# SwiGLU feed-forward of an encoder layer: seven products of half-matrix sums in place of eight, and a down projection of its own

## The chip, the cores and the metric

One core of a Trainium2 chip. The metric is the device time of one execution in microseconds (us), median of several runs. The engines of the core are TensorE (PE; its weight loads are listed as PEld), VectorE (DVE), ScalarE (ACT), GpSimd (POOL) and SyncE (SP), which only issues DMAs here. POOL issues DMAs too, on a queue of its own.

## The reference

One layer of a bidirectional encoder, in fp32, on 1536 tokens of 1024 channels: a prompt of 1024 tokens and a sample of 512 with the same weights.

```python
h  = rms_norm(x)                       # then w_in, two kinds of attention with 8 heads each
x  = x + concat(oA, oB) @ w_out
h2 = rms_norm(x)
x  = x + (silu(h2 @ w_gate) * (h2 @ w_up)) @ w_down     # 1024 -> 2816 -> 1024
y  = rms_norm(x)
```

## The kernel before

Every fp32 product is made of three passes in a faster fp32 format of PE: an operand is split into a high part (ACT rounds it, L125) and a low part (the operand less the high part, on DVE or POOL, L126), and `mm3` (L151 to L159, the matmul itself is L156) adds high x high, high x low and low x high in one bank of PSUM. PSUM has eight banks; `bank(kind, ...)` takes one of those that a kind shares.

The program runs in stages: projections and attention, interleaved, until some 812 us; the out-projection, tile by tile of 128 tokens, which also puts the residual into DRAM (`x2_d`, L837) and the norm's scale into `rs2`; then the feed-forward and the final norm. The change touches the last stage, from L942 on.

The feed-forward has two chunks of 768 tokens. `h2_tile` (L956) loads a tile of the residual, scales it (L963), transposes it on PE and splits it into `hh` and `hl`, [128, 8, 768]: channels on partitions, eight blocks of them. The first chunk's six tiles are made during the out-projection, the second's inside the first chunk's down projection. Then `gate_up(ck, f)` (L997 on) runs over the 22 blocks f of 128 hidden channels: weight tiles of 128 x 8 x 128 for gate and up, and for each half of the chunk (384 tokens) 8 x 3 matmuls of 384 columns for gate and as many for up, so 96 per block. ACT makes the silu (L1019), DVE multiplies (L1020), and the result is split into `hidh` and `hidl` (L1021, L1022), which stay in SBUF. After each group of two or three blocks (`GROUPS`), `down` (L1035 on) multiplies them by their rows of w_down: per tile of 128 tokens and half of the output (512 columns) 9 or 6 matmuls, and DVE adds the bank into the residual tile `x` (L1042). The weights come on POOL's queue (L137: gate and up, two units ahead; L987: w_down), and are loaded for each chunk. `finish` (L1044 on) is the final norm of a tile and its store on SP's queue (L1058, L1060).

The order on each engine is set by the program order of these calls and a scheduler that follows the tiles' dependences: an instruction waits on semaphores for its operands and for the buffers that its pool rotates. An engine works off its own instructions strictly in order, and so does each DMA queue's issuer.

## Time and profile before

| | us |
|---|---|
| median of 3 runs | 2038.98 |
| lowest and highest | 2035.26, 2049.47 |
| profiled execution: span of the trace | 2041.9 |
| first to last matmul of the feed-forward | 925.92 to 2032.23 |

Only the span is known of the profiled execution; it is 2.9 us above the median. Instructions are placed in us from the span's start. A matmul's listed duration overlaps that of its neighbours, so the pace of a run of matmuls is read from the distance of their starts. "Idle before" is time in which the engine stood still ahead of an instruction, with what ended it.

### The profile page before, as it was taken

What the parts mean: (1) busy time and instruction counts of PE and PEld (TensorE: products, weight loads), DVE (VectorE), ACT (ScalarE), POOL (GpSimd) and SP (SyncE); (2) the same over time, 40 slices, a digit from 0 to 9 for tenths busy, and PEclk for the clock granted to TensorE, in tenths of its full rate; (3) what the DMA queues carried; (4) which work ended last, traced back from release to release, by engine and by line L of the source; (5) the groups of instructions that cost most, each with busy time, mean ns of one, the idle gap of its engine ahead of it and who ended that gap; (6) DMA issues with size and microseconds to landing.
All of it is one profiled execution on the core that took longest, in us unless ns stands there. A gap on an engine that the chain in (4) does not pass through costs nothing.

```text
span 2041.9 us, 27504 instructions
## 1 busy us (share of the span) xinstructions
PE 1965.3 (96%) x10408; PEld 1662.7 (81%) x10408; DVE 1013.4 (50%) x2217; ACT 772.9 (38%) x1414; POOL 413.9 (20%) x445
## 2 busy tenths in 40 slices
PE   6999989999999979999999999999999999999998
PEld 5666666666666657889999999999899999999997
DVE  6566756667756676654333333333553333333325
ACT  5565655655566575443121121122331221221122
POOL 3323333343455521001010010010010100110100
PEclk9989998999999879999999999999999999999999
DMA  7788897898898897527122121221252211221201
GB/s 253 160 178 152 165 183 132 177 148 154 156 192 172 172 211 190 186 101 249 43 82 62 57 78 52 63 73 62 81 188 62 73 62 63 63 64 61 62 21 62
DMA packets 314293, 243.09 MB, mean 119 GB/s; under 512 B 259872, under 2 KB 271280, under 8 KB 314160
## 3 DMA queue, kind: packets, MB, share of 16 engines
q1 hardware_dynamic: 281424, 122.04, 29.6%
q0 software_dynamic: 32736, 119.30, 20.2%
q8 instruction: 81, 1.33, 0.3%
q14 instruction: 52, 0.43, 0.1%
HBM read 159.85 MB, written 21.14 MB: 89 GB/s over the span
## 4 chain that ended last, share of the span: by engine, by line
PE 86%; DMA 8%; DVE 2%; ACT 2%; issue 1%; SPq 1%; POOL 0%; DVEq 0%; ACTq 0%; POOLq 0%
PE acc L156 76%; DMA pT<-p 5%; PE sc L692 4%; PE pv L760 3%; PE sc L691 2%; DMA vna<-va 1%; PE pt L214 1%; ACT ka L504 0%; DMA bias_e<-in_rpbf_dram 0%; DMA taba<-e_d 0%; DVE p L745 0%; DMA wo_raw<-in_w_out_dram 0%; DVE htl L293 0%; DVE kb L508 0%; DMA x_sq<-in_x_prompt_dram 0%
## 5 line engine op out<-in xcount | busy, mean ns | idle before, releaser
L156 PE MATMUL acc<-hh,whi 128*128 128x384 f32 x1408 | 478.4, 340 | 0.0
L156 PE MATMUL acc<-hh,wlo 128*128 128x384 f32 x1408 | 474.9, 337 | 0.0
L156 PE MATMUL acc<-hl,whi 128*128 128x384 f32 x1408 | 474.5, 337 | 0.0
L156 PEld LDWEIGHTS acc<-hh,whi 128*128 128x128 f32 x1408 | 264.3, 188 | 0.6
L156 PEld LDWEIGHTS acc<-hl,whi 128*128 128x128 f32 x1408 | 264.3, 188 | 0.5
L156 PEld LDWEIGHTS acc<-hh,wlo 128*128 128x128 f32 x1408 | 264.7, 188 | 0.1
L156 PE MATMUL acc<-hth,whi 128*128 128x512 f32 x576 | 243.9, 424 | 3.4 <-ACT hth L290 1.5
L156 PE MATMUL acc<-htl,whi 128*128 128x512 f32 x576 | 241.2, 419 | 0.5 <-DVE htl L293 0.2
L125 ACT ACTIVATE whi<-wraw 128x1024 fp32r<-128x1024 f32 x136 | 143.5, 1057 | 258.1 <-PE acc L156 249.3
L156 PE MATMUL acc<-hth,wlo 128*128 128x512 f32 x576 | 241.1, 419 | 0.2 <-POOL wlo L126 0.2
L156 PE MATMUL acc<-wdh,hidh 128*128 128x512 f32 x528 | 206.0, 390 | 0.0
L156 PE MATMUL acc<-wdl,hidh 128*128 128x512 f32 x528 | 205.5, 389 | 0.0
L156 PE MATMUL acc<-wdh,hidl 128*128 128x512 f32 x528 | 205.5, 389 | 0.0
L1042 DVE TENSOR_TENSOR x<-acc,x 128x512 f32<-128x512 f32 x168 | 115.8, 690 | 164.5 <-PE acc L156 164.3
L1020 DVE TENSOR_TENSOR sl<-acc,sl 128x384 f32<-128x384 f32 x88 | 49.1, 557 | 280.2 <-PE acc L156 280.2
L739 ACT ACTIVATE t<-t,mt 128x768 f32<-128x768 f32 (+3 forms) x192 | 137.5, 716 | 124.2 <-DVE mt L732 121.3
L126 DVE TENSOR_TENSOR wlo<-wraw,whi 128x1024 fp32r<-128x1024 f32 x88 | 107.8, 1225 | 151.4 <-ACT whi L125 151.1
L745 DVE SCALAR_TENSOR_TENSOR p<-t,p 128x768 f16<-128x768 f32 (+3 forms) x192 | 145.5, 764 | 72.2 <-ACT p L741 71.8
L126 POOL TENSOR_TENSOR wlo<-wraw,whi 128x1024 fp32r<-128x1024 f32 x48 | 118.6, 2474 | 176.1 <-ACT whi L125 151.8
L741 ACT ACTIVATE p<-t 128x768 f16<-128x768 f32 (+3 forms) x192 | 118.1, 624 | 84.0 <-DMA pT<-p 54.4
L125 ACT ACTIVATE wdh<-wdr 128x1024 fp32r<-128x1024 f32 x44 | 45.3, 1054 | 273.4 <-PE acc L156 265.4
L156 PEld LDWEIGHTS acc<-hth,whi 128*128 128x128 f32 x576 | 113.0, 196 | 36.9 <-issue 9.2
(139 smaller groups left out, 2794.1 us busy)
## 6 DMA issues: line engine op xcount, KB each, us to landing
wraw<-in_w_in_dram POOLq DMA_DIRECT2D x46, 512.0 KB, 5.9
wraw<-in_w_gate_dram POOLq DMA_DIRECT2D x44, 512.0 KB, 4.5
wraw<-in_w_up_dram POOLq DMA_DIRECT2D x44, 512.0 KB, 4.5
wdr<-in_w_down_dram POOLq DMA_DIRECT2D x44, 512.0 KB, 4.2
tabb<-in_tabb_dram POOLq DMA_DIRECT2D x8, 800.0 KB, 6.2
x_d<-x_res SPq DMA_DIRECT2D x12, 512.0 KB
xh<-x_d SPq DMA_DIRECT2D x12, 512.0 KB
x<-x_d SPq DMA_DIRECT2D x12, 512.0 KB
```

The costliest lines, as they stand in the source:

```text
L125: return (nc.scalar.activation(hi, src, AF.Copy), eng.tensor_tensor(out=lo, in0=src, in1=hi.bitcast(F32), op=ALU.subtract))
L126: eng.tensor_tensor(out=lo, in0=src, in1=hi.bitcast(F32), op=ALU.subtract))
L156: latest[0] = nc.tensor.matmul(out=out, lhsT=a, rhs=b, start=i == 0, stop=i == last)
L214: nc.tensor.transpose(out=pts[k // 4][:, k % 4 * P:(k % 4 + 1) * P], in_=src[:, k * P:(k + 1) * P], identity=ident)
L691: nc.tensor.matmul(out=out, lhsT=qh[:, qs], rhs=kx, start=True, stop=False)
L692: nc.tensor.matmul(out=out, lhsT=qh[hs, qs], rhs=lx, start=False, stop=True)
L739: nc.scalar.activation(t, t, AF.Exp, bias=mt, scale=-1.0, accum_out=k.den)
L741: nc.scalar.activation(k.p16[:, 0], t, AF.Copy, scale=16384.0)
L745: nc.vector.scalar_tensor_tensor(out=k.p16[:, 1], in0=k.t, scalar=16384.0, in1=k.p16[:, 0], op0=ALU.mult, op1=ALU.subtract)
L760: nc.tensor.matmul(start=j + i == 0, stop=j + i == m, **one)
L1020: nc.vector.tensor_tensor(out=sl, in0=accs[1], in1=sl, op=ALU.mult)
L1042: nc.vector.tensor_tensor(out=xs[b][:, z], in0=acc, in1=xs[b][:, z], op=ALU.add)
```

## The change

A product of two matrices, each cut into 2 x 2 blocks, takes eight products of blocks; Strassen's scheme (here in Winograd's form) takes seven, of sums and differences of the blocks, and adds their results. Both matrix products of the feed-forward are rewritten so.

- Gate and up: the rows are the two halves of the 1024 channels, the columns of the weight matrix gate and up, the columns of the activations two halves of 384 tokens of the chunk. A step `u` is one block f of one chunk. Its seven products of 4 x 3 matmuls are issued in the order 1, 6, 2, 7, 5, 4, 3 into banks `mm`, `y` and `z` (two of each). POOL forms four weight sums per step (`w_sum`, L1046 on; tile `fs`), and ACT and DVE split seven weight blocks (L1061 is the low part). `h_sum` makes the seven activation operands of a chunk once (`h1h`, `h1l` to `h7h`, `h7l`; 128 x 1536 each, the low part on DVE at L1006, the sums on POOL). DVE adds the banks to the gate and up results.
- The weights come on SP's queue (`fw_load`), in three buffers `fraw` that gate and up share.
- After every second step POOL forms the sums of the hidden activations that the down projection wants (tile `as`, L1144), and SP writes all seven of them to DRAM (`hid_d`, L1145): 128 x 21 x 128, 1.38 MB in pieces of 512 bytes.
- The down projection runs after all steps: seven products, in the order 1, 7, 6, 4, 5, 2, 3, each over six pairs of token tiles b and eleven pairs of hidden blocks j, 33 matmuls of 512 columns per (n, b). The hidden operand is read back (`hraw`, 0.72 MB) and split again; pieces of w_down (`wq`, 256 KB, four buffers) come on SP's queue, are summed on POOL where the product wants it (`diff`), and split. Results are added into the residual tiles, which are loaded at the start (`x2`, twelve of 512 KB). `finish` follows for one tile of a pair in product 5, for the other in product 3.
- The pool of the old weights is released before the feed-forward.

```diff
-GROUPS = (3, 3, 3, 3, 3, 3, 2, 2)
-    wp = ctx.enter_context(tc.tile_pool(name="wp", bufs=1))
+    wp = tc.alloc_tile_pool(name="wp", bufs=1)
-    def mm3(out, ops):
+    def mm3(out, ops, first=True):
...
-                latest[0] = nc.tensor.matmul(out=out, lhsT=a, rhs=b, start=i == 0, stop=i == last)
+                latest[0] = nc.tensor.matmul(out=out, lhsT=a, rhs=b, start=first and i == 0, stop=i == last,
+                                              skip_group_check=not first)
...
-    kinds.update(mm=("mm", 2), pv=("pv", 2), dn=("dn", 4))
+    kinds.update(mm=("mm", 2), y=("y", 2), z=("z", 2), dn=("dn", 2))
...
+    def h_sum(n):
+        hi = hpool[n].tile([P, 4, HC], F32R, tag=f"h{n}h", name=f"h{n}h")
+        lo = hpool[n].tile([P, 4, HC], F32R, tag=f"h{n}l", name=f"h{n}l")
+        b11, b12, b21, b22 = raw[0, 0], raw[0, 1], raw[1, 0], raw[1, 1]
...
+        elif n == 5:
+            src = mix(b12, b22, b11, ALU.subtract)
+        elif n == 4:
+            src = mix(b21, b21, b11, ALU.subtract)
...
+        nc.scalar.activation(hi, src, AF.Copy)
+        nc.vector.tensor_tensor(out=lo, in0=src, in1=hi.bitcast(F32), op=ALU.subtract)
...
+    def fw_load(u):
...
+                t = fw.tile([P, NK, P], F32, tag="fraw", name="fraw", bufs=3)
+                nc.sync.dma_start(out=t, in_=w[:, f * P:(f + 1) * P].rearrange("(k p) f -> p k f", p=P))
...
+    def w_sum(u):
...
+        s1, s2 = temp(), temp()
+        add(s1, a21, a22, ALU.add)
+        parts(1, a11)
+        yield
+        add(s2, s1, a11, ALU.subtract)
+        yield
+        parts(6, s2)
...
+        parts(5, s1)
+        yield
+        parts(4, a22)
+        parts(3, s4)
...
+    def gate_up(u, extra=None):
...
+        fw_load(u + 2)
+        nxt = w_sum(u + 1)
+        x, y, z = (bank(tag, tag + "acc", HC) for tag in ("mm", "y", "z"))
+        for n in SEQ:
+            acc = {1: x, 2: x, 6: y, 7: y, 4: y, 5: z, 3: z}[n]
+            (wh, wl), (hh, hl) = wsum.pop((u, n)), hsum[n]
+            run(mm3(acc, [(wh[:, k], wl[:, k], hh[:, k], hl[:, k]) for k in range(4)], first=n in (1, 6, 5)))
...
+            next(nxt)
...
+        if odd:
+            A21 = a21.pop((ck, j))
+            for o, p, q, op in ((S1, A21, A22, ALU.add), (S2, S1, A11, ALU.subtract), (S3, A11, A21, ALU.subtract),
+                                (S4, A12, S2, ALU.subtract)):
+                nc.gpsimd.tensor_tensor(out=o, in0=p, in1=q, op=op)
+            nc.sync.dma_start(out=hid_d[:, ck, :, j], in_=a.rearrange("p n (c t) -> p (n c) t", t=P))
...
+    def piece(n, j):
+        lo = dp.tile([P, 512], F32R, tag="wlo", name="dlo", bufs=16)
+        hi = dp.tile([P, 512], F32R, tag="whi", name="dhi", bufs=16)
...
+            dst = dl.tile([P, 512], F32, tag="wq", name="wq", bufs=4)
...
+    def hid_load(n, b):
...
+        nc.sync.dma_start(out=z, in_=hid_d[:, ck, HN[n] * HT + c])
+        nc.scalar.activation(hi, z, AF.Copy)
+        nc.vector.tensor_tensor(out=lo, in0=z, in1=hi.bitcast(F32), op=ALU.subtract)
...
+        run(mm3(acc, [(hh[:, j], hl[:, j], *pieces[n, j]) for j in range(NP)]))
...
+        elif n == 6:
+            p = keep.pop(b)
+            add(p, acc)
+            for c in (c12, c21, c22):
+                add(c, p, nc.gpsimd)
```

DVE where the out-projection ends (`x_res` is its last addition, `rq..` are the small operations of the norm's scale, `wlo` a low part of a weight, `flo` and `h5l` low parts of a weight block and of an activation operand). Before:

```order
1510 L834 TENSOR_TENSOR x_res<-acc_9520,x_res 128x512
1511 L101 TENSOR_SCALAR rqx<-ss 128x1
1512 L102 TENSOR_SCALAR rqz<-rqx 128x1
1513 L103 TENSOR_SCALAR rqx<-rqx 128x1
1514 L105 TENSOR_SCALAR rqy<-rqx 128x1
1515 L109 SCALAR_TENSOR_TENSOR rqx<-rqz,rqy 128x1
1516 L126 TENSOR_TENSOR wlo<-wraw,whi 128x1024
```

And now:

```order
1506 L829 TENSOR_TENSOR x_res<-acc_9528,x_res 128x512
1507 L1006 TENSOR_TENSOR h7l<-q_9118,h7h 128x1536
1508 L1006 TENSOR_TENSOR h4l<-q_8742,h4h 128x1536
1509 L1006 TENSOR_TENSOR h3l<-q_9119,h3h 128x1536
1510 L100 TENSOR_SCALAR rqx<-ss 128x1
...
1517 L113 SCALAR_TENSOR_TENSOR rqy<-rqx,rqy 128x1
1518 L1006 TENSOR_TENSOR h5l<-q_9118,h5h 128x1536
1519 L108 SCALAR_TENSOR_TENSOR rqx<-rqz,rqy 128x1
1520 L1061 TENSOR_TENSOR flo<-fraw,fhi 128x512
```

The last row is the low part that the third matmul of the first product waits for: four low parts of activation operands and the norm's small operations now stand ahead of it. Before, the weights of the first block had been split earlier.

POOL inside a steady stretch of the feed-forward, where it only issued loads before:

```order
330 L137 DMA wraw<-in_w_up_dram 128x8x128
331 L137 DMA wraw<-in_w_gate_dram 128x8x128
332 L987 DMA wdr<-in_w_down_dram 128x1024 x3
333 L137 DMA wraw<-in_w_up_dram 128x8x128
334 L137 DMA wraw<-in_w_gate_dram 128x8x128
```

And now, the four weight sums each of two steps (`fs`), with the sums of hidden activations (`as`) between:

```order
469 L1065 TENSOR_TENSOR fs<-fraw 128x512
470 L1144 TENSOR_TENSOR as<-a_14066,as 128x384
471 L1065 TENSOR_TENSOR fs<-fs,fraw 128x512
472 L1065 TENSOR_TENSOR fs<-fraw 128x512
473 L1144 TENSOR_TENSOR as<-as 128x384 x2
474 L1065 TENSOR_TENSOR fs<-fraw,fs 128x512
475 L1065 TENSOR_TENSOR fs<-fraw 128x512
476 L1144 TENSOR_TENSOR as<-as,a_14363 128x384
477 L1065 TENSOR_TENSOR fs<-fs,fraw 128x512
478 L1065 TENSOR_TENSOR fs<-fraw 128x512
479 L1065 TENSOR_TENSOR fs<-fraw,fs 128x512
```

The loads are on SP's queue now, and POOL has arithmetic in their place. The first sum of a step has both operands in the up load, whose buffer the last sum of the step before sets free.

SP's queue between the feed-forward and the down projection (`x` the residual tiles, `wq` the first pieces of w_down, `hraw` the hidden operands read back). Before there was no such place. Now:

```order
527 L1145 DMA hid_d<-as 128x21x128
528 L1187 DMA wq<-in_w_down_dram 128x512 x4
529 L1255 DMA x_16353<-x_d 128x1024
...
535 L1255 DMA x_16539<-x_d 128x1024
536 L1145 DMA hid_d<-as 128x21x128
537 L1255 DMA x_16541<-x_d 128x1024
...
541 L1255 DMA x_16671<-x_d 128x1024
542 L1217 DMA hraw<-hid_d 128x1408 x2
543 L1187 DMA wq<-in_w_down_dram 128x512 x4
```

The first residual load (row 529) waits on a semaphore of PE for the last matmul of the feed-forward. The last hidden block is written behind seven residual loads, and the first hidden operand is read behind five more.

## Rows read from the trace of the kernel before

**Rows 1.** The page: the span, the engines' busy time (share of the span, instructions), the rate of the DMAs in 40 equal slices, and the chain of work that ended last, by line:

```profile
span 2041.9 us, 27504 instructions
PE 1965.3 (96%) x10408; PEld 1662.7 (81%) x10408; DVE 1013.4 (50%) x2217; ACT 772.9 (38%) x1414; POOL 413.9 (20%) x445
...
GB/s 253 160 178 152 165 183 132 177 148 154 156 192 172 172 211 190 186 101 249 43 82 62 57 78 52 63 73 62 81 188 62 73 62 63 63 64 61 62 21 62
...
PE acc L156 76%; DMA pT<-p 5%; PE sc L692 4%; PE pv L760 3%; PE sc L691 2%; DMA vna<-va 1%; PE pt L214 1%; ACT ka L504 0%; DMA bias_e<-in_rpbf_dram 0%; DMA taba<-e_d 0%; DVE p L745 0%; DMA wo_raw<-in_w_out_dram 0%; DVE htl L293 0%; DVE kb L508 0%; DMA x_sq<-in_x_prompt_dram 0%
```

**Rows 2.** Busy time of each engine in three windows inside the feed-forward (us from the span's start, length, then per engine busy us and instructions; granted clock, busy share of the DMA engines, GB/s):

```profile
930.00:990.00 60.00, 60.00 (x344) 60.00 (x342) 23.30 (x32) 18.86 (x26) 10.11 (x14) 1.00 0.58 202
1000.00:1100.00 100.00, 100.00 (x517) 92.70 (x516) 35.06 (x46) 18.42 (x25) 8.09 (x11) 1.00 0.19 58
1600.00:1800.00 200.00, 200.00 (x1046) 187.34 (x1045) 68.05 (x90) 39.20 (x55) 17.50 (x22) 1.00 0.19 58
```

**Rows 3.** The timeline of PE in the feed-forward: start us, us, engine, line, operation, number. First the first matmul of the stage, then the 2nd and the 32nd, then two of the old down projection, 54 apart:

```profile
925.92 0.34 PE L156 MATMUL acc<-hh,whi 128*128 128x384 f32 x1
926.10 0.33 PE L156 MATMUL acc<-hl,whi 128*128 128x384 f32 x1
...
931.36 0.34 PE L156 MATMUL acc<-hl,whi 128*128 128x384 f32 x1
...
999.69 0.39 PE L156 MATMUL acc<-wdl,hidh 128*128 128x512 f32 x1
...
1011.93 0.39 PE L156 MATMUL acc<-wdl,hidh 128*128 128x512 f32 x1
```

**Rows 4.** PE's instructions from 925 to 2033 us by line and shape: number, busy us, mean ns of one (they overlap, so the pace is that of the starts), idle before. For each of the two products one of three rows with the same number stands here:

```profile
L156 PE MATMUL acc<-hh,whi 128*128 128x384 f32 x1408 | 478.4, 340 | 0.0
...
L156 PE MATMUL acc<-wdh,hidl 128*128 128x512 f32 x528 | 205.5, 389 | 0.0
L214 PE MATMUL pt<-ident,xh 128*128 128x128 f32 x48 | 6.2, 272 | 0.0
```

**Rows 5.** DVE's and ACT's groups by line and shape, whole span: number, busy us, mean ns of one, idle before and what ended it:

```profile
L1042 DVE TENSOR_TENSOR x<-acc,x 128x512 f32<-128x512 f32 x168 | 115.8, 690 | 164.5 <-PE acc L156 164.3
L126 DVE TENSOR_TENSOR wlo<-wraw,whi 128x1024 fp32r<-128x1024 f32 x88 | 107.8, 1225 | 151.4 <-ACT whi L125 151.1
L1020 DVE TENSOR_TENSOR sl<-acc,sl 128x384 f32<-128x384 f32 x88 | 49.1, 557 | 280.2 <-PE acc L156 280.2
L1022 DVE TENSOR_TENSOR hidl<-sl,hidh 128x384 fp32r<-128x384 f32 x88 | 48.8, 555 | 26.6 <-ACT hidh L1021 26.6
L125 ACT ACTIVATE whi<-wraw 128x1024 fp32r<-128x1024 f32 x136 | 143.5, 1057 | 258.1 <-PE acc L156 249.3 <-DMA wraw<-in_w_in_dram 7.6 <-issue 1.1
L125 ACT ACTIVATE hh<-pt 128x512 fp32r<-128x512 f32 x24 | 13.7, 594 | 39.0 <-PE pt L214 39.0
L1019 ACT ACTIVATE sl<-acc 128x384 f32<-128x384 f32 x88 | 42.5, 483 | 135.4 <-PE acc L156 135.4
```

**Rows 6.** POOL and DVE side by side near 500 us (timeline of the one and of the other), then line L293, whole span: engine, number, min/median/max ns, first and last start, shapes:

```profile
499.92 2.52 POOL L126 TENSOR_TENSOR wlo<-wraw,whi 128x1024 fp32r<-128x1024 f32 x1
...
499.85 0.68 DVE L732 CUSTOM_DVE_ANT_0 t<-sc,tabb 128x512 f32<-128x512 f32 x1
...
500.68 0.48 DVE L732 CUSTOM_DVE_ANT_1 t<-sc,tabb,mt 128x256 f32<-128x256 f32 x1
...
501.09 1.92 DVE L293 TENSOR_TENSOR htl<-xhalf,hth 128x512 fp32r<-128x512 f32 x1
...
L293 DVE TENSOR_TENSOR htl<-xhalf,hth x8: 660/684/1916, 480.1 to 514.4; 128x512 fp32r<-128x512 f32 x8
L293 POOL TENSOR_TENSOR htl<-xt,hth x4: 1272/1286/1827, 36.3 to 48.0; 128x512 fp32r<-128x512 f32 x4
```

**Rows 7.** All DMA engines busy near the start of the program (a window, columns as in rows 2), then the issues of two weight loads: queue, number, KB each, median us from issue to landing:

```profile
15.00:21.00 6.00, 5.09 (x10) 3.12 (x11) 5.96 (x7) 4.44 (x7) 5.22 (x4) 1.00 1.05 399
...
wraw<-in_w_gate_dram POOLq DMA_DIRECT2D x44, 512.0 KB, 4.5
wdr<-in_w_down_dram POOLq DMA_DIRECT2D x44, 512.0 KB, 4.2
```

**Rows 8.** The timeline of PE where it starts after an idle time, matmuls of 512 columns:

```profile
15.71 0.80 PE L156 MATMUL acc<-hth,whi 128*128 128x512 f32 x1 [1.50 <-ACT hth L290]
...
17.57 0.63 PE L156 MATMUL acc<-hth,whi 128*128 128x512 f32 x1
18.00 0.63 PE L156 MATMUL acc<-htl,whi 128*128 128x512 f32 x1
...
21.90 0.39 PE L156 MATMUL acc<-hth,whi 128*128 128x512 f32 x1
22.13 0.39 PE L156 MATMUL acc<-htl,whi 128*128 128x512 f32 x1
```

**Rows 9.** The end of the timeline of all engines, from the last matmul on:

```profile
2032.23 0.39 PE L156 MATMUL acc<-wdh,hidl 128*128 128x512 f32 x1
...
2034.78 0.15 DVE L1051 TENSOR_TENSOR ss<-ss 128x1 f32<-128x1 f32 x1
...
2037.85 0.99 SPq L1058 DMA_DIRECT2D out_dram<-x  x2
```

More of the change, by code (lines that the diff above doesn't have):

```diff
@@ L187, in hymba_layer_kernel @@
     n_in = len(units)
-    for ck in range(2):
-        for f in range(NFF):
-            for w in (w_gate, w_up):
-                units.append(w[:, f * P:(f + 1) * P])
     hp = tc.alloc_tile_pool(name="hp", bufs=2)
@@ L208, in transposed, with transposed_whole @@
         dst(pt)
-    def transposed_whole(src, hi, lo):
-        pts = [bank("dn", "pt2") for _ in range(2)]
+    def transposed_whole(src, put, tag="dn"):
+        pts = [bank(tag, "pt2") for _ in range(2)]
         for k in range(NK):
@@ L972, in hymba_layer_kernel @@
         if 4 <= i < 10:
-            h2_tile(0, i - 4, late, "xh", g_f)
+            raw_tile(0, i - 4, late, "xh", 1, "yz"[i % 2])
+        if i == 9:
+            for n in (1, 6, 2):
+                h_sum(n)
     late.release()
@@ new lines, in w_sum, with temp, parts, add @@
+    def w_sum(u):
+        if u >= len(steps):
+            while True:
+                yield
+        g, up = wraw.pop(u)
+        a11, a12, a21, a22 = g[:, :4], g[:, 4:], up[:, :4], up[:, 4:]
+        def temp():
+            return fw.tile([P, 4, P], F32, tag="fs", name="fs", bufs=4)
+        def parts(n, src):
+            hi = fw.tile([P, 4, P], F32R, tag="fhi", name="fhi", bufs=8)
+            lo = fw.tile([P, 4, P], F32R, tag="flo", name="flo", bufs=8)
+            nc.scalar.activation(hi, src, AF.Copy)
+            nc.vector.tensor_tensor(out=lo, in0=src, in1=hi.bitcast(F32), op=ALU.subtract)
+            wsum[u, n] = (hi, lo)
+        def add(o, a, b, op):
+            nc.gpsimd.tensor_tensor(out=o, in0=a, in1=b, op=op)
+        s1, s2 = temp(), temp()
[5 more added lines that the diff above has]
+        parts(6, s2)
+        yield
+        parts(2, a12)
+        s3 = temp()
+        add(s3, a11, a21, ALU.subtract)
+        yield
+        parts(7, s3)
+        s4 = temp()
+        add(s4, a12, s2, ALU.subtract)
+        yield
+        parts(5, s1)
+        yield
+        parts(4, a22)
+        parts(3, s4)
+        yield
@@ new lines, in hymba_layer_kernel @@
+    a21 = {}
+    fw_load(0)
+    fw_load(1)
+    first = w_sum(0)
+    for n in range(7):
+        next(first)
+        if n >= 3:
+            h_sum(SEQ[n])
+    for u, (ck, f) in enumerate(steps):
+        last = ck == 0 and f == NFF - 1
+        gate_up(u, h_sum if last else None)
+        if ck == 0 and f >= 5 and f % 2 and f // 2 - 2 < CT:
+            raw_tile(1, f // 2 - 2, fp, "xh", 1, "dn")
+    fp.release()
+    hB.release()
+    fw.release()
+    rq.release()
+    hA.release()
+    rot = [0]
@@ L1047, in finish @@
+    order = [(n, b) for n in WSEQ for b in range(NB)]
+    hid_load(*order[0])
+    for j in range(NP):
+        piece(1, j)
+        if j == 4:
+            hid_load(*order[1])
+    diff = dl.tile([P, NP, 512], F32, tag="diff", name="diff")
+    g_o = dl.tile([P, D], F32, tag="go", name="g_o")
+    nc.gpsimd.dma_start(out=g_o, in_=g_final.partition_broadcast(P))
+    xs, keep = {}, {}
+    def finish(i, x, last=False):
+        junk = dl.tile([P, D], F32, tag="junk", name="junk3", bufs=1)
         ss = small.tile([P, 2], F32, tag="ss2", name="ss2")
@@ L1062, in hymba_layer_kernel @@
[L1062 to L1088 removed]
+            nc.sync.dma_start(out=dst, in_=x)
```

263 lines of the change are left out of this document (159 added, 104 removed).

## The prediction

> **What bounds the kernel now.** I read the page's busy times first: TensorE (PE) is busy 96% of a span of 2041.9 us, and 76% of the chain that ended last is the one matmul line L156 [rows 1]. The stage that the change touches is then cut out with the windows view. In three windows of the feed-forward PE is busy for the whole window, at a granted clock of 1.00 (2.4 GHz), while DVE is busy 34 to 39% of it, ACT 18 to 31%, and the DMA engines 0.19 to 0.58 [rows 2]. The starts of single matmuls give the pace: 30 products of 384 columns from 926.10 to 931.36 are 0.1755 us each, 54 of 512 columns from 999.69 to 1011.93 are 0.2267 us each [rows 3]. Their counts are 3 x 1408 and 3 x 528, with 48 transposes of 6.2 us together [rows 4]: 4224 x 0.1755 + 1584 x 0.2267 + 6.2 = 741.3 + 359.1 + 6.2 = 1106.6 us. The stage lasts from 925.92 [rows 3] to the last matmul at 2032.23 plus 0.39 [rows 9], 1106.7 us. So it holds no stall, and each matmul taken out is worth its pace, until another engine or a transfer is late.
>
> **What goes.** A step (one block of 128 hidden channels, one chunk of 768 tokens) has 7 x 4 x 3 = 84 matmuls of 384 columns where it had 96: 44 x 12 = 528 fewer, 92.7 us. The down projection has 7 x 6 x 11 x 3 = 1386 of 512 where it had 1584: 198 fewer, 44.9 us. Together 137.6 us, and 2041.9 - 137.6 = 1904.3 us is the floor. Of 168 additions of 0.69 us on DVE after the old down products [rows 5] 54 are left there; PE waited for none, so this counts for nothing.
>
> **What comes, by places.**
>
> Start of the feed-forward. On DVE three low parts of activation sums (128x1536) now stand between the last addition of the out-projection and the first weight split, with a fourth behind the small operations of the norm; the third matmul of the first product waits for that split. From 1.225 us for 128x1024 [rows 5] one is 1.83: 4 x 1.83 + some 8 small ones at 0.15 [rows 9] + 0.69 = 9.2 us, of which the last out-projection matmuls hide little. GpSimd (POOL) forms two of the sums meanwhile, 3 x 1.29 = 3.9 us each by its 128x512 row [rows 6]; if one is late, its length is added. Bounds 7 and 18, taken 12. The out-projection tiles get three such sums more on a DVE that had slack: 1 (0 to 2).
>
> Steady step. Its period on PE is 84 x 0.1755 = 14.74 us. ACT: 7 splits of 128x512 (0.60) and 3 of 384 (0.48) = 5.6 us [rows 5]. DVE: 7 low parts at 0.684 [rows 6], 2 products of 384 columns from SBUF at 0.555, 5 additions from PSUM at 0.557 [rows 5] = 4.8 + 1.1 + 2.8 = 8.7. POOL: 4 sums of 128x512 at 1.29 [rows 6] and on average 2 of 384 columns, 0.97 by columns, = 7.1. Each alone fits. But do DVE and POOL run side by side? Near 500 us POOL has a subtraction from 499.92 to 502.44; DVE's operations that read one operand from PSUM take 0.68 and 0.48 beside it, then the low part L293, both operands in SBUF, takes 1.92, where its median is 0.684, and ends 0.57 after POOL does [rows 6]. So such a pair goes one after the other. Then 4.8 + 1.1 + 7.1 = 13.0 us of a step are serial, and with DVE's PSUM work, if none of it falls beside POOL, 15.8: 1.06 us over the period, 47 us in 44 steps. Bounds 0 and 47; as DVE and POOL both wait at times, some of the 2.8 will fall beside POOL, so I take 0.3 us a step, 13 us. PE's own order gives the splits room: products 1, 6 and 5 of the next step are issued before 4 and 3 of this one, some 36 matmuls or 6.3 us after their parts can be made.
>
> The Trainium skill, page "SBUF — State Buffer", section "Who interferes with whom", says the same more sharply: a VectorE instruction with two SBUF inputs and a GpSimd instruction that reads SBUF share one port pair under an exclusive lock, and whichever starts second is blocked until the first ends. This trace agrees (1.92 against 0.684 us). It speaks against this change, which moves weight and activation sums to just that engine; without the rule and the row the step would have been costed at nothing.
>
> The turn to the second chunk: four activation sums again, interleaved with the last step; only the last wait, for two low parts and a POOL sum, should reach PE. Taken 5, bounds 2 (one low part) and 10 (two POOL sums and a low part).
>
> From feed-forward to down projection. The SBUF of the old stage has to come free, so the twelve residual loads of 512 KB wait for PE's last matmul, all on SP's queue; the last hidden block (1.38 MB, in pieces of 512 bytes) is written after the seventh of them, and the first hidden block is read (0.72 MB) behind the twelfth. The last block's own chain (DVE 0.56, ACT 0.48, DVE 0.56, three POOL sums at 0.97) runs beside the first loads. 6.29 + 1.38 + 0.72 = 8.4 MB must pass: 21 us at 399 GB/s, the rate with all engines busy at 15 to 21 us [rows 7], 42 us at the 202 GB/s of 930 to 990 us [rows 2]. The queue will be full, so the first rate is nearer: 21, then the landing, the split on ACT (1408 columns from 1.057 for 1024: 1.45) and the low part on DVE (1.68): 27 us. Bounds 15 (if the read overtakes) and 44. PE idles through it. After the idle start of the program PE goes at 0.43 us a matmul of 512 columns [rows 8], about half its pace, for some 6 us: 3 us more, bounds 0 and 6.
>
> Down projection. A product of one sum and six column blocks lasts 6 x 33 x 0.2267 = 44.9 us. Seven of the first eleven weight pieces arrive through four buffers while PE already works on two accumulators: 3 (0 to 8). Then, per 44.9 us, DVE has 11 low parts (7.5), 6 of 1408 columns (10.1) and 6 to 12 additions (4.1 to 8.3); POOL 11 sums (14.2): serial at most 40, hidden. In the product n=6 POOL has 18 additions besides: 29 x 1.29 = 37.4, with 17.6 of DVE's that exclude it 55.0, 10 us too long; bounds 0 and 14 (with 4.1 of PSUM additions). The tail behind the last matmul stays as it is, 9.3 us [rows 9].
>
> Sum: 1904.3 + 12 + 1 + 13 + 5 + 27 + 3 + 3 + 10 = 1978.3 us as a profiled execution, which before was 2.9 us above the median of 2038.98. Forecast 1975 us. With all lower ends, 1904.3 + 7 + 2 + 15 - 2.9, 1925; with all upper ones, 1904.3 + 18 + 2 + 47 + 10 + 44 + 6 + 8 + 14 - 2.9, 2050.
>
> **Rivals.**
> A, everything hides and only the two drains remain at their lower ends: 1925 to 1935, say 1930. For it: DVE and ACT stand idle two thirds of the old stage [rows 2]. Against it: the 8.4 MB behind PE's last matmul, and the row on the two engines. Chance 0.2.
> B, the down stage is bound by its traffic: while n=7 and n=5 are prepared, 6 x 0.72 + 22 x 0.26 = 10.1 MB must come in 44.9 us, 225 GB/s; five others need 7.2 or less, 160. If 160 is what one queue with waits gives, two phases take 63 us: 36 more, 2011. For it: 35 of the 40 slices of the span stay under 190 GB/s; against it: 253 and 249 in two of them, 399 in a short window [rows 1, 7]. Chance 0.1.
> C, slower than before: the loop of POOL and weight loads sets the step. The up load of a step waits for the fourth sum of the step before (three buffers), the next first sum waits for that load, and each second time the hidden write stands ahead of it in SP's queue. For two steps: 14.2 us of POOL, two landings of 4.5 us [rows 7], the write at 3.4 (399 GB/s) to 6.8 us (202), less 1.3 that it overlaps: 25.3 to 28.7, under the 29.5 of PE. But if each of the 12 POOL sums also waits out one low part of 0.69, it is 33.6 to 37.0; at 35.3 it costs 5.8 us for each of 22 pairs, 128 us in place of my 13: 2090. It decides from 29.5 on, and is slower than before from 33 on. Against it: DVE is idle for 6 us of a step, so few sums meet a low part. Chance 0.1.
> The forecast case has 0.6.
>
> **How the numbers follow.** A measurement here tells about 1% from no change, 2018.6 to 2059.4. Faster: nearly all of A, the forecast case but its upper tail, and B mostly: 0.2 + 0.53 + 0.07 = 0.8. Same: the tail of the forecast case, B's and C's weak form: 0.1. Slower: C, 0.1. The range 1922 to 2045 goes from A's end to near the forecast case's upper one and leaves out C.
>
> **What would show it.** Right: 3696 and 1386 matmuls at 0.1755 and 0.2267 us; gaps of about 12 us on PE at the first step, 27 at the start of the down stage, DVE low parts with a mean well over 0.69 us in the feed-forward, a little idle PE in a steady window, more in the n=6 product. Wrong: a steady window with PE at 100% and low parts at 0.69 (A); PE under 90% there, waiting for low parts whose sums waited for an up load (C); PE waiting for hidden reads or weight pieces in the n=1 and n=4 products at 160 GB/s (B); a gap at the turn far from 27, or matmuls at another pace.

## The result and the profile after

The changed kernel takes 1982.45 us (median of five runs, 1980.49 to 1998.44). The kernel before, run on the same chip in between, takes 2035.26 (2029.27 to 2049.47). The ratio is 0.9745, 95% interval 0.9692 to 0.9798: faster, by 52.8 us. The forecast was 1975 with a range of 1922 to 2045.

The profiled execution of the changed kernel lasted 1998.44 us, 16 above the median. Most of that lies ahead of the changed stage, in the attention part: the last matmul of the out-projection starts at 935.41 us, where the kernel before has 925.69. That moment lies between 908 and 936 us in the profiles of this study. So kernels are compared by their **stage**, from the start of the last out-projection matmul to the start of the last matmul of all. It lasted 2032.23 - 925.69 = 1106.5 us before [rows 9] and 1987.74 - 935.41 = 1052.3 after, 54.2 less; the tail behind it was 9.7 us and is 8.9.

The page of the kernel after: span, and busy time of each engine with its share of the span and instructions, to be held against [rows 1]:

```profile
span 1996.6 us, 27529 instructions
PE 1844.1 (92%) x9682; PEld 1539.6 (77%) x9682; DVE 1319.6 (66%) x2532; ACT 922.3 (46%) x1673; POOL 825.6 (41%) x647
```

PE is busy for 121 us less, POOL for 412 more, and the stage is only 54 us shorter: PE now waits, and the windows show where. Windows of the kernel after (columns as in [rows 2]: from:to, length, then busy us and instructions of PE, PEld, DVE, ACT, POOL; granted clock, DMA share, GB/s):

```profile
938.00:955.00 17.00, 4.08 (x12) 3.58 (x13) 16.76 (x20) 7.54 (x12) 12.39 (x5) 0.50 0.51 139
...
960.00:1260.00 300.00, 299.22 (x1727) 298.25 (x1726) 215.69 (x290) 120.57 (x208) 176.88 (x121) 1.00 0.42 121
1260.00:1310.00 50.00, 42.12 (x204) 40.12 (x203) 47.37 (x40) 23.44 (x33) 34.19 (x17) 0.86 0.28 80
1310.00:1610.00 300.00, 299.36 (x1715) 299.23 (x1715) 205.87 (x285) 112.49 (x200) 174.06 (x122) 1.00 0.41 116
1610.00:1648.00 38.00, 11.67 (x64) 10.89 (x62) 11.63 (x16) 5.80 (x10) 5.65 (x5) 0.69 0.85 308
1648.00:1730.00 82.00, 72.83 (x293) 58.40 (x292) 48.86 (x43) 27.97 (x38) 42.44 (x27) 0.92 0.71 239
```

The two steady stretches of 300 us hold 0.8 and 0.6 us of idle PE. The loss stands in four places: the first step, the turn to the second chunk (1260 to 1310), the gap before the down projection, and the down projection's first 130 us. In each of them the granted clock is below 1.00.

The timeline of PE after, at these places (start us, us, operation, number, in brackets the idle time before it and what ended it):

```profile
935.41 0.39 PE L155 MATMUL acc<-wo_h,ol 128*128 128x512 f32 x1
945.22 0.69 PE L155 MATMUL mmacc<-h1h,fhi 128*128 128x384 f32 x1 [9.43 <-ACT fhi L1060]
...
951.92 0.69 PE L155 MATMUL mmacc<-h1h,flo 128*128 128x384 f32 x1 [5.69 <-DVE flo L1061]
...
1305.29 0.69 PE L155 MATMUL yacc<-h7h,fhi 128*128 128x384 f32 x1 [4.56 <-DVE u L1115]
...
1647.36 0.79 PE L155 MATMUL acc<-dhi,dhh 128*128 128x512 f32 x1 [25.68 <-ACT dhh L1218]
...
1649.62 0.63 PE L155 MATMUL acc<-dhi,dhh 128*128 128x512 f32 x1
1650.04 0.63 PE L155 MATMUL acc<-dlo,dhh 128*128 128x512 f32 x1
...
1713.64 0.80 PE L155 MATMUL acc<-dhi,dhl 128*128 128x512 f32 x1 [5.90 <-DVE dhl L1219]
...
1766.05 0.80 PE L155 MATMUL acc<-dhi,dhl 128*128 128x512 f32 x1 [4.43 <-DVE dhl L1219]
```

The counts are those of the forecast: 21 groups of 176 matmuls of 384 columns (3696) and three of 462 of 512 (1386). One of the 21, by line and shape:

```profile
L155 PE MATMUL mmacc<-h1h,fhi 128*128 128x384 f32 x176 | 60.9, 346 | 10.0 <-ACT fhi L1060 10.0
```

DVE's and POOL's groups after, by line and shape (number, busy us, mean ns of one, idle before), which answer to [rows 5, 6]:

```profile
L1061 DVE TENSOR_TENSOR flo<-fs,fhi 128x512 fp32r<-128x512 f32 x176 | 155.9, 886 | 56.7 <-ACT fhi L1060 54.6 <-PE mmacc L155 2.1
L1061 DVE TENSOR_TENSOR flo<-fraw,fhi 128x512 fp32r<-128x512 f32 x132 | 138.2, 1047 | 45.2 <-ACT fhi L1060 45.2
...
L1207 DVE TENSOR_TENSOR dlo<-diff,dhi 128x512 fp32r<-128x512 f32 x33 | 41.3, 1303 | 5.5 <-ACT dhi L1206 5.5
```

```profile
L1065 POOL TENSOR_TENSOR fs<-fraw 128x512 f32<-128x512 f32 x88 | 131.8, 1498 | 234.8 <-DMA fraw<-in_w_up_dram 219.3 <-DVE flo L1061 7.8 <-DVE as L1136 5.9
```

A low part of 128x512 takes 0.89 to 1.30 us on average against the 0.684 it takes alone, a sum on POOL 1.50 against 1.29 [rows 6]: where they run side by side, both engines pay.

### The profile page after: what moved, and what is told of

The parts are those of the page before. It is cut to its first block, busy times and chain, and to the rows that moved or that the text cites. A ratio compares the mean times of both kernels' runs of the same rounds, so it can differ in the third digit from the quotient of the medians.

```text
span 1996.6 us, 27529 instructions
## 1 busy us (share of the span) xinstructions
PE 1844.1 (92%) x9682; PEld 1539.6 (77%) x9682; DVE 1319.6 (66%) x2532; ACT 922.3 (46%) x1673; POOL 825.6 (41%) x647
## 4 chain that ended last, share of the span: by engine, by line
PE 53%; DVE 6%; DMA 5%; ACT 2%; issue 1%; POOL 1%; SPq 0%; DVEq 0%; ACTq 0%; POOLq 0%
PE acc L155 22%; PE yacc L155 12%; PE mmacc L155 9%; PE zacc L155 8%; DMA pT<-p 2%; DVE dlo L1207 1%; DMA vna<-va 1%; DVE flo L1061 1%; DVE dhl L1219 1%; PE pt L210 1%; DVE rqx L108 1%; PE sc L687 1%; DMA fraw<-in_w_up_dram 1%; POOL as L1144 0%; DMA hraw<-hid_d 0%
## 5 line engine op out<-in xcount | busy, mean ns | idle before, releaser
L1065 POOL TENSOR_TENSOR fs<-fraw 128x512 f32<-128x512 f32 x88 | 131.8, 1498 | 234.8 <-DMA fraw<-in_w_up_dram 219.3
L155 PE MATMUL acc<-dhi,dhh 128*128 128x512 f32 x462 | 182.8, 397 | 28.2 <-ACT dhh L1218 28.2
L1060 ACT ACTIVATE fhi<-fs 128x512 fp32r<-128x512 f32 x176 | 110.7, 630 | 202.2 <-PE yacc L155 64.6
L155 PE MATMUL acc<-dhi,dhl 128*128 128x512 f32 x462 | 183.7, 398 | 13.6 <-DVE dhl L1219 13.6
L1061 DVE TENSOR_TENSOR flo<-fs,fhi 128x512 fp32r<-128x512 f32 x176 | 155.9, 886 | 56.7 <-ACT fhi L1060 54.6
L155 PE MATMUL acc<-dlo,dhh 128*128 128x512 f32 x462 | 182.3, 395 | 0.0
L1061 DVE TENSOR_TENSOR flo<-fraw,fhi 128x512 fp32r<-128x512 f32 x132 | 138.2, 1047 | 45.2 <-ACT fhi L1060 45.2
L155 PEld LDWEIGHTS acc<-htl,whi 128*128 128x128 f32 x576 | 113.4, 197 | 31.4 <-issue 6.4
L155 PEld LDWEIGHTS acc<-hth,wlo 128*128 128x128 f32 x576 | 113.5, 197 | 31.1 <-issue 6.4
L155 PEld LDWEIGHTS acc<-dhi,dhh 128*128 128x128 f32 x462 | 88.8, 192 | 47.7 <-ACT dhh L1218 29.4
```

Source lines behind the costliest of these rows:

```text
L155: latest[0] = nc.tensor.matmul(out=out, lhsT=a, rhs=b, start=first and i == 0, stop=i == last, skip_group_check=not first)
L1060: nc.scalar.activation(hi, src, AF.Copy)
L1061: nc.vector.tensor_tensor(out=lo, in0=src, in1=hi.bitcast(F32), op=ALU.subtract)
L1065: nc.gpsimd.tensor_tensor(out=o, in0=a, in1=b, op=op)
```

## The experiments

Each kernel is the changed one with the edit shown. "Stage" is as above; the changed kernel has 1052.3 us.

**The changed kernel once more**, nothing edited.

> The changed kernel once more, nothing edited. Theory 1 (the stage from the last out-projection matmul to the last matmul repeats, and what varies between profiled executions lies ahead of it): 1052.3 us within 2, with the waits of the first trace, 15 us at the start, 8 at the turn, 26 at the start of the down projection, 16 in it, none in the steady windows. Theory 2 (the stage itself varies): it differs by 4 us or more, and differences of a few us between the other runs can't be read.

Measured: 1988.52 us (ratio 0.9752, 0.9717 to 0.9788), stage 1050.9. PE's waits up to the down projection repeat: 15.1 us at the start, 9.4 at the turn (8.5 in the first trace), 26.2 at the gap. Those inside the down projection do not: they are 10.5 us in place of 15.7, with 2.2 where the first trace has 5.90. So theory 1 holds for the stage, which repeats within 1.5 us while the span differs by 4.3, but not for every wait. By these two runs, differences of some 4 us between stages can be read, differences of a few us between the waits of the down projection can't.

**The residual loads on another queue.** The forecast put the gap of 27 us down to 8.4 MB in one queue.

```diff
-            nc.sync.dma_start(out=hid_d[:, ck, :, j], in_=a...)
+            wr = nc.gpsimd if u == len(steps) - 1 else nc.sync
+            wr.dma_start(out=hid_d[:, ck, :, j], in_=a...)
...
-                nc.sync.dma_start(out=xs[i], in_=x2_d[i * P:(i + 1) * P, :])
+                nc.gpsimd.dma_start(out=xs[i], in_=x2_d[i * P:(i + 1) * P, :])
```

> The twelve residual loads of the down stage (12 x 512 KB) and the last write of a hidden block go through POOL's queue instead of SP's; nothing else is changed. Theory 1 (order in one queue): the 25.7 us wait of PE before the down projection is the time in which the first hidden operand stands behind 6.3 MB of residual loads and the 1.4 MB write in SP's queue. With those on another queue its read starts at once and shares the DMA engines with them: 1.44 MB at half of about 360 GB/s is 8 us, less what overlaps the last step, plus 1.4 and 1.7 us of splitting: the wait falls to 8 to 13 us, the time by 13 to 18 us. Rival (the amount, not the order): the 8.4 MB have to come anyway at some 360 GB/s, and the wait stays at 20 to 26 us; the time by 0 to 5 us.

Measured: 1986.74 us (0.976, 0.9707 to 0.9814), stage 1057.5, and the gap grew from 26 to 30 us. The timelines of POOL and of ACT in this kernel (x now stands on POOL ahead of everything else):

```profile
1598.29 4.68 POOL L1256 DMA_DIRECT2D x<-x_d  x9 [4.42 <-PE zacc L155]
...
1610.14 1.47 POOL L1146 DMA_DIRECT2D hid_d<-as  x1 [0.30 <-POOL as L1144]
```

```profile
1626.66 2.64 ACT L1219 ACTIVATE dhh<-hraw 128x1408 fp32r<-128x1408 f32 x2 [25.38 <-DMA hid_d<-as]
```

POOL issues all twelve loads before it makes the last hidden sums, so the write is issued 12.5 us after the start of the last matmul of the steps (1597.65), where it was 6.5, and ACT, which waits for that write, starts 16.5 us after its issue: its output lies where the hidden sums lay. The read, on SP's queue, had been issued at 1607.73, before that write. So the edit freed the read and delayed the write, and the write became the limit. Both theories' numbers failed, and what the order of SP's queue costs was not yet told apart.

**The residual loads held back**, on the same queue: each tile's load waits, by a copy of one column into the tile, until the hidden operand has been split.

```diff
                 xs[i] = dl.tile([P, D], F32, tag="x2", name="x2", bufs=NT)
+                nc.vector.tensor_copy(out=xs[i][:, :1], in_=hids[n, b][0][:, 0, :1].bitcast(F32))
                 nc.sync.dma_start(out=xs[i], in_=x2_d[i * P:(i + 1) * P, :])
```

> The changed kernel, with a copy of one column on DVE ahead of each residual load of the down stage, taken from the hidden operand of the same column block, so that these loads can't be issued before that operand is there. All loads stay in SP's queue. In the last run (residual loads and last write on POOL's queue) the wait stayed, because the buffer of the split operand is that of the hidden sums and so waits for the landing of their write too. Theory 1 (order in the queue): now only the 1.4 MB write stands ahead of the read, so the wait is the chain of the last hidden block, 6 us, then about 5 us for the write, 2 for the read, 2 until it lands, and the split: 15 to 18 us in place of 25.7; from the last out-projection matmul to the last of all 1052.3 us becomes 1040 to 1044. Rival (amount): the residual is only put off and comes in the way of weight pieces, the wait falls but the first product waits for pieces by as much: 1050 to 1055.

Measured: 1979.09 us (0.9742, 0.9703 to 0.9781), stage 1040.7, the gap 16.4 + 0.4 us. SP's queue in the changed kernel, and then in this one:

```profile
1621.72 3.28 SPq L1255 DMA_DIRECT2D x<-x_d  x7
1627.82 0.37 SPq L1145 DMA_DIRECT2D hid_d<-as  x1
1628.24 8.50 SPq L1255 DMA_DIRECT2D x<-x_d  x5
1636.84 0.85 SPq L1217 DMA_DIRECT2D hraw<-hid_d  x2
```

```profile
1621.81 0.38 SPq L1145 DMA_DIRECT2D hid_d<-as  x1
1622.29 4.21 SPq L1217 DMA_DIRECT2D hraw<-hid_d  x2
```

In the changed kernel the longest wait, 25.7 us, is made of 6.1 until the write is issued, 9.0 until the read is, behind five of the residual loads, and 10.5 until the first matmul; here the 16.4 are 6.1, 0.5 and 9.8. The stage is 11.6 us shorter (10.2 against the repeat), 9.3 of them by the gap, and of these 8.5 by the earlier issue of the read. Theory 1 holds: the loads ahead in the queue are shown to be the cause of that part. The loads did not cost it back later, as the rival had it, for the waits inside the down projection are 12.0 us here. The other 16 us are the last block's own chain, the write and the read.

**The sums of w_down pieces on DVE**, so that POOL's subtraction no longer runs beside the low parts of the down projection.

```diff
-            nc.gpsimd.tensor_tensor(out=o, in0=a, in1=b, op=op)      # in piece()
+            nc.vector.tensor_tensor(out=o, in0=a, in1=b, op=op)
```

> The sums of the w_down pieces (4 of the 7 products have them) are made on DVE instead of POOL; the three additions of product 6 stay on POOL. Theory 1 (shared port): the waits of 5.9, 4.4 and some 2 us at the turns between products come from DVE's low parts (10 in 14.8 us, 1.48 each instead of 0.68) taking turns with POOL's sums. With no POOL sum beside them a low part takes 0.69, and even with the sums (0.69 each) on DVE the burst is some 10 us: the waits in the down stage fall from 16 us to under 6, and the stretches at half clock behind them go: 10 to 18 us faster. Rival (DVE is simply too busy there): DVE has 44 sums more, some 30 us, so the waits grow to 20 us or more: 5 to 10 us slower.

Measured: 1971.09 us (0.9679, 0.9626 to 0.9732), stage 1043.8, 8.6 shorter (7.1 against the repeat). PE waits 8.4 us inside the down projection, where the changed kernel had 15.7 and its repeat 10.5. The group of low parts in this kernel:

```profile
L1207 DVE TENSOR_TENSOR dlo<-diff,dhi 128x512 fp32r<-128x512 f32 x33 | 23.5, 750 | 0.7 <-ACT dhi L1206 0.7
```

DVE has the 44 sums as well, and a low part takes 0.75 us, not 1.30. So theory 1 is right in the cause and in the direction, but the gain is under its 10 to 18 us, and the waits are above its 6.

**All sums of the feed-forward on DVE** (weights, activations, hidden), so that POOL has none.

```diff
-            nc.gpsimd.tensor_tensor(out=o, in0=a, in1=b, op=op)      # w_sum; alike in h_sum and after a step pair
+            nc.vector.tensor_tensor(out=o, in0=a, in1=b, op=op)
```

> All sums of the gate and up part (weights, activations, hidden activations) are made on DVE instead of POOL; the down stage is as it was. Theory 1 (shared port, hidden in the steady steps): DVE has 8.7 + 4 x 0.69 + 2 x 0.52 = 12.5 us of work in a step of 14.74, low parts at 0.69 instead of 0.89 to 1.05, and PE stays at 100% in the steady windows; the start of the feed-forward loses its POOL sum of 4.9 us and the low part of 5.0 us beside it, so its waits fall from 15.1 to about 10 us, and those at the turn to the second chunk from 7.9 to about 4: 6 to 12 us faster with the clock's part. Rival (POOL takes work off DVE that PE would wait for): a DVE at 85% or more delays the additions from PSUM, PE falls to 97% or less in the steady windows: 10 to 30 us slower.

Measured: 1979.13 us (0.9722, 0.9673 to 0.9771), stage 1057.3, 4.9 longer. In this kernel the low parts, PE's waits in all, and a steady window read:

```profile
L1061 DVE TENSOR_TENSOR flo<-fs,fhi 128x512 fp32r<-128x512 f32 x176 | 120.6, 686 | 22.8 <-ACT fhi L1060 22.6
```

```profile
PE mmacc L155 <- ACT fhi L1060: 14.3, 31, 7.8
```

```profile
938.00:1238.00 300.00, 296.85 (x1693) 291.85 (x1691) 232.32 (x405) 114.64 (x202) 0.00 (x0) 1.00 0.41 119
```

The low part is at 0.686 us in all 176: the stretching was POOL's. The first step's waits fall from 15.1 to 8.8 us. But PE now loses some 3 us in 300 of a steady stretch, which it did not before: 31 waits for a high part (the longest, 7.8 us, is the start's), while DVE stands in its own order before a sum whose up load has not landed. Each theory had a part of it right.

**Weight sums twice on POOL**: the same result, double the work.

```diff
-            nc.gpsimd.tensor_tensor(out=o, in0=a, in1=b, op=op)      # in w_sum
+            for _ in range(2):
+                nc.gpsimd.tensor_tensor(out=o, in0=a, in1=b, op=op)
```

> Each of the four weight sums of a step is made twice on POOL (the same result written again). It asks how far the steady step is from its next limit. By my forecast's figures DVE's two-operand work and POOL's exclude each other: 5.9 + 12.3 = 18.2 us for a step of 14.74, so 3 to 4 us more per step, 130 to 180 us slower, with PE waiting for low parts. By the loop of POOL and weight loads: 14.2 + 10.3 + 11 = 36 us or more for two steps instead of 29.5, some 140 us slower, with POOL waiting for the up load and PE for its sums. If neither binds (both run side by side, 12.3 us on POOL): no more than 10 us.

Measured: 2099.07 us in one run, stage 1164.7, 112 longer. Windows of this kernel, and its longest wait:

```profile
960.00:1260.00 300.00, 269.59 (x1472) 255.05 (x1470) 202.69 (x247) 91.43 (x174) 233.07 (x171) 0.99 0.35 102
```

```profile
PE yacc L155 <- ACT fhi L1060: 49.4, 24, 4.0
```

The price is 112 / 44 = 2.5 us a step, less than either forecast had. All weight sums take 508.4 us of POOL in place of 277.0, 5.3 us more a step, so some 3 us of them were covered. By this estimate that is the distance of the changed kernel's steady step from its next limit. Which limit it is was not told apart. PE at 90% and waiting for high parts of POOL's sums is rival C's picture. But PE also waits 32 us, in 31 places, for low parts, which the exclusion alone would bring too, and POOL waits 68 us in all for up loads, where the changed kernel has 219.

**Three edits together**: residual loads held back, sums of w_down and of activation operands (h_sum) on DVE.

> Three edits together: sums of the w_down pieces on DVE (1043.8 us from the last out-projection matmul to the last of all when alone), the residual loads held back, and the sums of the activation operands (at the two starts) on DVE, while the weight and hidden sums of the steady steps stay on POOL. Theory 1: the start loses the POOL sum and the stretched low part as it did with all sums on DVE (waits 15.1 to 8.8 us), the steady steps stay without waits as before, the gap before the down stage is 15 to 18 us: 1023 to 1030, a time of 1950 to 1960. Rival (the edits share one cause, a wait removed at one place returns at the next): 1036 or more.

Measured: 1967.75 us (0.9666, 0.9626 to 0.9705), stage 1035.1, between the two forecasts. The start's waits fall to 11.0 us and the gap to 16.6, but the steady windows are no longer full. The second of them in this kernel:

```profile
1303.00:1603.00 300.00, 294.12 (x1674) 291.76 (x1674) 202.36 (x282) 111.93 (x199) 163.21 (x119) 1.00 0.41 113
```

With the 3.6 us of the first, 9.4 of 600 us are idle, in waits of 0.6 to 1.3 us. Two edits without the third tell where these come from.

**Two edits**: residual loads held back, sums of w_down on DVE.

> The sums of w_down pieces on DVE and the residual loads held back, as in two runs before, but the sums of the activation operands stay on POOL. Theory 1 (parts add up; the short waits in the steady steps of the three-edit kernel, 0.6 to 1.1 us every second step, come from the sums of the activation operands on DVE): the stage from the last out-projection matmul to the last matmul is 1052.3 - 8.6 - 11.6 = 1032 us (1030 to 1034), the first step waits about 15 us again, PE stands nowhere in the steady windows, ratio to before about 0.965. Theory 2 (those short waits come with the other two edits or with the run, not with those sums): they are here too, and the stage is 1038 us or longer, since the start's 5 us are lost without anything for them.

Measured: 1968.28 us (0.9654, 0.9625 to 0.9684), stage 1030.7. Theory 1 holds. The same window in this kernel, against which the first has 1.0 us of idle PE:

```profile
1302.00:1602.00 300.00, 299.40 (x1715) 299.06 (x1715) 204.36 (x284) 111.83 (x201) 171.59 (x123) 1.00 0.42 116
```

The two gains of 11.6 and 8.6 us add up (1052.3 - 20.2 = 1032.1), and the activation sums on DVE, not the other edits, bring the short waits. Why a change at the chunk's start still shows in later steps was not settled. This kernel has the shortest stage of the study, and is faster than the kernel before and the changed kernel once more, which ran on the same chip (1968.28 us against 2039.67 and 1988.52).

**The last residual write on POOL's queue**, on top of the three edits: the first step's weight loads then no longer stand behind it on SP.

```diff
-        nc.sync.dma_start(out=x2_d[i * P:(i + 1) * P, :], in_=xt)
+        (nc.gpsimd if i == NT - 1 else nc.sync).dma_start(out=x2_d[i * P:(i + 1) * P, :], in_=xt)
```

> The three edits, and the last residual tile's write to DRAM on POOL's queue, so that the first weight loads don't stand behind it in SP's queue (it waits for the last addition of the out-projection, and they were issued 0.0 us after it). Theory 1: the first split then waits for no load; the first wait of PE falls from some 8 to 3 to 5 us: 3 to 6 us less than with the three edits alone. Rival: the first weight split stands behind the last activation operand on ACT, and that behind a sum on DVE, so the load was not last: within 1 us of the three edits.

Measured: 1968.04 us (0.9687, 0.9645 to 0.9729), stage 1034.7, 0.4 less than without it, as the rival had it. The start still waits 8.9 + 4.1 us, where the three edits alone have 7.8 + 2.0 + 1.2. ACT's timeline in this kernel, whose last out-projection matmul starts at 908.72 us:

```profile
915.94 1.49 ACT L1005 ACTIVATE h5h<-q 128x1536 fp32r<-128x1536 f32 x1 [3.12 <-DVE q L991]
917.33 0.61 ACT L1060 ACTIVATE fhi<-fraw 128x512 fp32r<-128x512 f32 x1
```

The weights' loads are issued before 902.3 us now, and the first split of a weight (fhi) still comes at 917.33: it stands in ACT's order behind the high part of an activation sum, which waits for the sum.

**Matmuls to fill the gap**: 56 matmuls into an unused bank, on top of the three edits, so that PE comes to the down projection from work and not from idleness.

```diff
+    hot = any_bank()
+    for _ in range(56):
+        nc.tensor.matmul(out=hot, lhsT=pieces[1, 0][1][:, :P], rhs=pieces[1, 0][0], start=True, stop=True)
```

> The three edits, and 56 matmuls of 512 columns on two weight parts that are already there, into a bank that nothing reads, between the last product of the feed-forward and the first of the down stage: PE has 12.7 us of work in a gap of 15 to 18. Theory 1 (a wait also costs PE its clock): the granted clock stays at 2.4 GHz, the first matmuls of the down stage go at 0.227 instead of 0.43 us, and the stage is 2 to 4 us shorter than with the three edits alone. Rival (the first matmuls are slow for another reason, their weights or the queue): no difference.

Measured: 1966.78 us in one run, stage 1036.3, 1.2 longer. PE's timeline:

```profile
1629.17 0.39 PE L155 MATMUL acc<-dhi,dhh 128*128 128x512 f32 x1
1629.39 0.39 PE L155 MATMUL acc<-dlo,dhh 128*128 128x512 f32 x1
...
1641.62 1.22 PE L155 MATMUL acc<-dhi,dhh 128*128 128x512 f32 x2 [5.80 <-ACT dhi L1206]
...
1643.92 0.63 PE L155 MATMUL acc<-dhi,dhh 128*128 128x512 f32 x1
1644.35 0.63 PE L155 MATMUL acc<-dhi,dhl 128*128 128x512 f32 x1
```

The first matmuls of the down projection now go at 0.23 us and not at 0.43. After 24 of them PE waits 5.80 us for the ninth weight piece, and goes on at 0.43. But the edit also changed PE's order, and so it is no clean test of what the clock is worth. In the three-edit kernel the matmuls of the first two token pairs alternate from the 15th on, so PE has the second pair's to do until that piece is there; here the first pair's 24 matmuls for eight pieces come first. The ninth piece is split as late after the first matmul in both (12.0 us there, 11.8 here). The run shows the pace after a filled gap; neither forecast of the time is settled by it.

## Why the prediction was right, and which term was not

By steps, in us of the stage (the floor is 1106.5 - 137.6 = 968.9; after lasted 83.4 more):

| step of the sum | forecast | measured |
|---|---|---|
| start of the feed-forward | 12 (7 to 18) | 9.43 + 5.69 = 15.1 |
| steady step, 44 times | 13 (0 to 47) | about 1 |
| turn to the second chunk | 5 (2 to 10) | 8.5 in six waits, the longest 4.56 |
| gap before the down projection | 27 (15 to 44) | 25.68 + 0.44 = 26.1 |
| first pieces, product n=6 | 3 + 10 (0 to 22) | 15.7: 2.8 in n=1, 5.9 in n=7, 4.4 in n=6, 2.5 in n=5 |
| clock after idleness | 3 (0 to 6) | 17.0, what is left of the 83.4 |
| sum | 73 | 83.4 |

The out-projection tiles, costed at 1, took 2.2 us of waits and lie ahead of the stage. That the total is so near is luck in part: the two largest misses, -12 and +14, cancel. The floor and the gap, which carry most of it, were right by themselves.

**Right.** The matmuls removed are worth their pace: 3696 and 1386 remain, and the steady stretch of 1310 to 1610 us goes at 299.36 / 1715 = 0.1746 us a matmul (0.1755 forecast). The gap has the size and the cause given: from 1621.7 to 1645.9 us, when the hidden operand has landed, the DMA engines move 362 GB/s (399 forecast). Holding the residual loads back took 9.3 us out of it and not the 15.8 that their 6.29 MB have in the forecast's sum, since the last block's chain of 6.1 us, which had run beside the first of them, then stands alone.

**The term of the clock was mis-sized.** The forecast counted one restart, at the down projection. There some nine matmuls go at 0.43 us and not 0.23, which is 2 of its 3 us. But every wait of some us has such a restart, and the forecast listed waits at five other places without this price. Windows around the changes of product in the down projection of the kernel after (columns as above):

```profile
1713.00:1722.00 9.00, 8.36 (x24) 6.68 (x25) 6.13 (x6) 0.00 (x0) 7.41 (x5) 0.63 0.67 216
1722.00:1760.00 38.00, 38.00 (x169) 31.47 (x168) 22.22 (x20) 13.34 (x16) 10.25 (x7) 1.00 0.43 138
...
1766.00:1775.00 9.00, 8.95 (x30) 7.19 (x31) 2.73 (x3) 0.00 (x0) 6.36 (x4) 0.73 0.62 221
```

After the wait of 5.90 us the granted clock is 0.63 on average (a part at 1.2 GHz, the rest at 2.4), and 24 matmuls take 8.36 us: at 0.2267 they would take 5.4, so the wait cost 2.9 us more than itself. After that of 4.43 us, 30 take 8.95 and not 6.8: 2.1 more. The turn, with six waits in 33 us, has 0.86 over its 50 us. Summed over all places by the distances of single starts the excess is some 19 us; the faster steady pace gives 3696 x 0.0009 = 3.3 back. That leaves some 16, near the 17.0 of the table. The run with matmuls in the gap shows it from the other side: without the idleness ahead the first matmuls are at full pace, and after a wait of 5.80 us they are not.

**The steady step was overestimated.** DVE and POOL do exclude each other there, as the forecast argued from the 1.92 us row [rows 6]: the low parts are stretched to 0.89 and 1.05, and are at 0.686 once POOL has no sums. POOL is busy 174 of 300 us, 8.6 per step of 14.7 in place of the forecast 7.1, DVE 205.9, 10.1 in place of 8.7. But PE waits for nothing: no engine reaches the step's length, and PE's order gives the splits the 6 us of room that the forecast itself had named. The step that failed is "0.3 us a step", a value taken between bounds whose lower end was 0. Doubling POOL's sums shows where the room ends, some 3 us of POOL work further on. What decides there, rival C's loop or the exclusion alone, that run does not tell.

**The start and the turn were a little underestimated**, by the same exclusion. The timelines of DVE, POOL and ACT in the kernel after, at the first step and (DVE's last rows) at the turn:

```profile
939.78 4.97 DVE L1006 TENSOR_TENSOR h3l<-q,h3h 128x1536 fp32r<-128x1536 f32 x1
...
1298.04 5.05 DVE L1006 TENSOR_TENSOR h4l<-q,h4h 128x1536 fp32r<-128x1536 f32 x1
...
1304.69 0.55 DVE L1115 TENSOR_TENSOR u<-yacc,p 128x384 f32<-128x384 f32 x1
```

```profile
938.27 4.87 POOL L991 TENSOR_TENSOR q<-q,q 128x1536 f32<-128x1536 f32 x1 [16.41 <-DVE h7l L1006]
```

```profile
943.17 1.48 ACT L1005 ACTIVATE h5h<-q 128x1536 fp32r<-128x1536 f32 x1 [3.60 <-POOL q L991]
944.56 0.61 ACT L1060 ACTIVATE fhi<-fraw 128x512 fp32r<-128x512 f32 x1
```

POOL's sum takes 4.87 us, not the 3.9 of the forecast, and ends at 943.14; ACT waits for it, makes h5h, and only then the weight's high part for which PE stands until 945.22. The low part h3l beside that sum takes 4.97 us where the one ahead of it took 1.75, and PE's second wait follows from it down DVE's order. The forecast had followed DVE alone and added POOL only "if one is late". At the turn h4l takes 5.05 us, and the addition u, for which PE waits 4.56 us, stands behind it.

**In the product n=6 the cause was wrong.** The prediction feared POOL's 18 additions there. They take 1.77 us each on average, and PE waits for none of them. Its one wait in that product, 4.43 us at the second token pair, ends at 1766.05, before the first of them begins:

```profile
1767.27 5.08 POOL L1263 TENSOR_TENSOR x<-keep,x 128x512 f32<-128x512 f32 x3 [3.36 <-DVE keep L1263]
```

That wait and the one of 5.90 us, at the second token pair of product 7, have another cause: POOL sums the pieces of the product after and DVE takes their low parts. DVE and POOL after, ahead of the wait of 5.90 us:

```profile
1696.16 14.83 DVE L1207 TENSOR_TENSOR dlo<-diff,dhi 128x512 fp32r<-128x512 f32 x10
1710.91 2.68 DVE L1219 TENSOR_TENSOR dhl<-hraw,dhh 128x1408 fp32r<-128x1408 f32 x1
```

```profile
1696.98 15.12 POOL L1191 TENSOR_TENSOR diff<-diff,wq 128x512 f32<-128x512 f32 x9 [2.84 <-DMA wq<-in_w_down_dram]
```

Ten low parts at 1.48 us alternate with nine sums at 1.68, and the hidden low part that PE needs next stands behind them in DVE's order. So the prediction was right to count POOL's work and DVE's together, but what decides is how much of it stands ahead of one operand, not whether it fits into a product of 44.9 us. The Trainium skill, page "SBUF — State Buffer", section "Who interferes with whom", has the rule: a VectorE instruction with two SBUF inputs and a GpSimd instruction that reads SBUF share a port pair under an exclusive lock. This trace agrees in the main: a low part takes 1.48 us beside POOL's sums, 0.684 alone and 0.75 once the sums are on DVE. It also shows that a serial count is an upper bound. Ten low parts and nine sums are done in 15.9 us, where one after the other at 0.684 and 1.29 they would take 18.5.

**The rivals.** A (all hides but the drains) has the full steady window that it asked for, though with low parts far from 0.69 us; its time failed at the edges. B did not come at its price: the window 1648 to 1730 moved 239 GB/s, above the 225 that it asked for. But its sign is there in small. The 2.8 us in product 1 and the 2.5 us in product 5 are waits for a hidden operand that stands, in ACT's order, behind splits of weight pieces that had not landed, or whose sums had waited for them: 5.3 us in place of B's 36. C did not come.

## What to carry to other kernels

Work taken off the full engine was worth its whole pace in the steady part, even though the two helpers that took on the extra work exclude each other, because each step had room; the price was paid at the edges, where a stage fills or drains, so count those one by one and look at what stands ahead in each queue. Price each wait of a few us on PE with its restart, 2 to 3 us here after 4 to 6 us of waiting. Before moving a transfer to another queue, ask who issues it and what its landing releases; holding it back on the same queue was worth 11.6 us here, moving it cost 5.1, each within some 1.5 us.
